# A two-layer encoder on one core: mixer A's empty step taken out, a query split put one step later, and the last half's plain units spread and brought forward

## The chip, the core and the metric

The kernel runs on one core of a Trainium2 chip. The core has a matrix engine (PE in the profile; its weight loads are PEld), a vector engine (DVE), a scalar engine (ACT), a general engine (POOL) and a sync engine (SP) that issues most of the DMAs. Each engine takes its own instructions in order and waits on semaphores for the others. The time is that of one execution in device microseconds. Of the kernel before there are three timed runs and one profiled execution.

## The reference

One sequence of 256 positions, model width 2048, in float32, goes through two layers. Each layer is `h = h + mixer(rms_norm(h))`, then `h = h + conv_ffn(rms_norm(h))`; at the end stands one more RMS norm.

```python
def mixer_a(h, w_qkv, w_o, q_gain, k_gain):      # layer 0
    qkv = h @ w_qkv                               # 16 query heads, 4 key and 4 value heads of 128
    q, k = axial_rope(rms_norm(q, q_gain)), axial_rope(rms_norm(k, k_gain))
    p = softmax(q @ k.T * 128 ** -0.5)            # every query sees every key; 4 query heads share a key head
    return (p @ v) @ w_o

def mixer_b(h, w_qkv, w_o, rel_bias):             # layer 1: 3 groups of 8 heads
    ...                                           # strided windows (128,1), (512,4), (2048,16), a bias by distance
    y = wts[g] * outs[g]                          # groups weighted by their softmax denominators
    return y @ w_o

def conv_ffn(h, w_up, conv_w, conv_b, w_down):
    u = conv3(h @ w_up) + conv_b                  # width 3, one filter for each of 2 x 5632 channels
    gate, val = split(u, 2)
    return (silu(gate) * val) @ w_down
```

The activations are small and the weights are not: nearly all of the work is products of 256 rows with weights that are read once from memory.

## The kernel before

**Products.** Weights come in blocks of 128 x 1024 numbers (512 KB) into one of six `raw` buffers. Each block is split in two: ACT makes the rounded high part `wh` (L128), DVE the rest `wl` (L129, L165 where it goes by halves), both in buffers from a ring of three (four in the down-projection). A product is then three matmuls: high by high, high by low and low by high. A block serves twelve matmuls of 512 columns where it is used plainly. The two splits are moved ahead in the order of the work by 45 instructions (`AHEAD`), so that DVE and ACT take them before other work that is ready.

**Order of the work.** The program is written as one sequence. Helpers that have to run beside the products are Python generators in a list `pending`: after each block, `step()` resumes the first of them up to its next `yield`, and when one ends, the next one is resumed in the same step. A scheduler then makes one in-order queue for each engine; it takes the written order as priority, and takes what it holds to be ready by its own account of durations. So a `yield` more or less moves everything of that generator, and of those behind it, by one block of the product that runs beside it, but the order on an engine need not be exactly the written one.

**Mixer A.** For each of four groups of four query heads, `project` makes the queries from eight blocks (eight steps). Behind it `attend(g)` is started: `qk_post` normalises and rotates the queries (ACT L793 and L903 read the product's banks, DVE L905, L912, L913, POOL L910, and POOL's power at L454 gives the factors `rqk`, which DVE scales at L937). Three steps later PE transposes the queries (L810), ACT and DVE split them into `qTh` and `qTl` (L303, L304). Then come six steps, k = 0 to 5: at k = 0 to 3 the scores of head k are made and their softmax begun ("S", L320 to L322 with `kT` and `qT`, DVE L957, L959, L966, L968, ACT L963), at k = 1 to 4 the probabilities of head k-1 are transposed ("T", L976) and split into `pTh` and `pTl`, and at k = 2 to 5 the output of head k-2 is made ("V", L320 to L322 with `v` and `pT`) and split into the attention's slots `ah` and `al`. Two heads share one bank for V, so the second one's product waits until the first one's output has been read. Between the query split and k = 0 the first group, and it alone, has an empty step; because each generator starts where the one before ends, all four groups keep that place against the products.

**Mixer B.** Six passes (two halves of the heads, three groups) make keys and queries with a Strassen-Winograd scheme (`seven`, seven products in place of eight). Behind each, `k_gen` and `s_gen` turn the keys and queries with the vector engine: a transposition in 32 x 32 blocks (L348), then sixteen block copies, eight on POOL (L358) and eight on ACT (L360), in two steps; one step later, for the first group alone, ACT and DVE split the result into `qTh` and `qTl` (`heads_T_dve`, L303 and L304). After two more steps the scores begin.

**The feed-forward.** The 5632 channels go through in two halves, six and five groups of 512. In the down-projection of a half, the columns are taken in pairs of 512 (0 and 1, then 2 and 3). `weave` writes the order of a pair's units. A plain unit ("c") takes one block and makes twelve matmuls on C11 and C21 (columns n0) or on C12 and C22 (columns n1). A Winograd unit ("P") makes six, from a block that has often been added to another one by DVE first (L248); seven P's do the work of eight c's on one group of channels. The first pair of a half (`late`) begins with LEAD = 4 plain units, because the last group of channels is still being made; at its first use the program empties `pending` (`drain`). After the last P, `combine` (nine operations, ACT L475 and DVE L476 to L487) brings the four product banks M1, M5, M6, M7 into `h`; `done` adds C11 and C21, later C12 and C22 to `h` (DVE L649), and in the last half ACT sums squares (L651) and POOL multiplies by the final gain (L652). All eight banks are in use, and the second pair uses the same ones. The last pair of all (`tail`) has one Winograd group and ends with a plain feed of four products for each bank (L153 to L155), after which the final norm and the stores follow.

Of the kernel before, what the change touches and what calls it, by code (L numbers as in the profile page):

```python
# [28 lines left out]
LEAD = 4  # L29
# [4 lines left out]
def tile_encoder(ctx: ExitStack, tc: tile.TileContext, x, xT, w_a, w_ao, q_gain, k_gain, w_b, w_bo,  # L34
# [34 lines left out]
    def ps_tile():  # L69
        bank_at[1] = (bank_at[1] + 1) % 4  # L70
        return bank(4 + bank_at[1], "ps")
# [12 lines left out]
    def start(gen):  # L84
        if next(gen, StopIteration) is not StopIteration:
            pending.append(gen)
# [414 lines left out]
    def ffn(l, hT, ss_in, g_next, last, side=None):  # L501
        with tc.tile_pool(name=nm("wpool"), bufs=1) as wp, tc.tile_pool(name=nm("fpool"), bufs=1) as fp:
# [101 lines left out]
            for hf, (p0, p1) in enumerate(HALVES):  # L604
# [83 lines left out]
                if last and hf == 1:  # L688
                    for n in range(4):
                        f = hpool.tile([P, 512], F32, tag=f"x{n}", name=nm("fin"))  # L690
                        nc.gpsimd.dma_start(f, final_norm[n * 512:(n + 1) * 512].partition_broadcast(P))
                        fin.append(f)
                def weave(lead, tail):
                    ks = SKG[hf][:1] if tail else SKG[hf]
                    c = [("c", k, i) for k in range(np_) if k not in ks for i in range(4)]
                    ps = [("P", k, p) for k in ks for p in ORDER]
                    if tail:
                        c0, c1 = ([u for u in c if u[2] // 2 == n] for n in range(2))
                        c = c0[:-1] + c1[:3] + c0[-1:] + c1[3:-2]
                    units = []  # L700
                    units += [c.pop(0) for _ in range(lead)]
                    lone = (ps[0], ps[7]) if lead > 1 and hf == 0 else ()
                    for u in ps:
                        units += [u] + [c.pop(0) for _ in range(min(1, len(c))) if u not in lone]
                    return units + c

                hl_ring.insert(0, (wp, 9))
# [8 lines left out]
                    done((a["C11"], a["C21"]), n0)  # L716

                def pair(n0, n1, late, tail=False):
                    units = weave(LEAD if late else 1, tail)
                    late_at = next(i for i, u in enumerate(units) if u[1] == np_ - 1)  # L720
                    acc = project_pair(wd, n0, n1, slots, forms.get, units, late_at if late else None,
                                       lambda a: start(combine(a, n0, n1, fp, "s", combined)),
                                       lambda a: first_half(a, n0, n1), tail=tail)
                    accs = acc["C12"], acc["C22"]
                    if tail:
                        feed(accs, slots, np_ - 1, wd[n1, np_ - 1], False, True, True)
                    done(accs, n1)
                    finished(n0, n1)
# [83 lines left out]
            hi, lo = (v[:, 2 * hp:2 * hp + 2, :].rearrange("p a c -> p (a c)") for v in o)  # L812
            split(hi, lo, t)

    def heads_T_dve(o, s, pool, tag, place="pava"):
        hi, lo = o
        dst = hi if lo is None else s.rearrange("p m c -> p (m c)").rearrange("p (j t) -> p j t", j=4)
        yield from turned(dst, s, pool, tag, place)
        yield
        if lo is not None:  # L820
            split(hi, lo, dst)

    def mixer_a():
        with tc.tile_pool(name="apool", bufs=1) as ap:
# [110 lines left out]
            def attend(g, accs):  # L935
                ro, rq = qk_post(accs, "q")
                nc.vector.tensor_scalar(rq, rq, SCALE, None, op0=ALU.mult)  # L937
                rqv = rq.rearrange("p (m a) -> p m a", m=2)
                qT = pair_tile(ap, [P, 4, NT], "qT")
                yield  # L940
                yield
                yield
                for _ in heads_T(qT, ro):
                    pass
                if g == 0:
                    yield
                prs, pTs, ots = {}, {}, {}
                for k in range(6):
                    yield
                    if k < 4:  # L950
                        i = k
                        s = ps_tile()
                        for m in range(2):
                            mm3(s[:, m * NT:(m + 1) * NT], qT, kT,
                                (slice(None), i, slice(m * P, (m + 1) * P)), (slice(None), g), True, True)
                        mx = small.tile([P, 2], F32, tag="mx", name=nm("mx"), bufs=3)
                        nc.vector.tensor_reduce(mx, s.rearrange("p (m c) -> p m c", m=2), axis=AX.X,  # L957
                                                op=ALU.max, negate=True)
                        nc.vector.tensor_tensor(mx, mx, rqv[:, :, i], ALU.mult)  # L959
                        pr = ap.tile([P, 2, NT], F32, tag="pr", name=nm("pr"), bufs=2)  # L960
                        l = small.tile([P, 2], F32, tag="l", name=nm("l"), bufs=3)
                        for m in range(2):
                            nc.scalar.activation(pr[:, m, :], s[:, m * NT:(m + 1) * NT], AF.Exp,  # L963
                                                 bias=mx[:, m:m + 1], scale=rq[:, 4 * m + i:4 * m + i + 1],
                                                 accum_out=l[:, m:m + 1])
                        nc.vector.reciprocal(l, l)  # L966
                        for m in range(2):
                            nc.vector.tensor_scalar(pr[:, m, :], pr[:, m, :], l[:, m:m + 1], None, op0=ALU.mult)  # L968
                        prs[i] = pr
                    if 1 <= k < 5:  # L970
                        i = k - 1
                        pr = prs.pop(i)
                        t = ps_tile()
                        for m in range(2):
                            for kt in range(2):
                                nc.tensor.transpose(t[:, kt * NT + m * P:kt * NT + (m + 1) * P],  # L976
                                                    pr[:, m, kt * P:(kt + 1) * P], ident)
                        pTs[i] = pair_tile(ap, [P, 2 * NT], "pT", 2)
                        split(pTs[i][0], pTs[i][1], t)
                    if k >= 2:  # L980
                        i = k - 2
                        pT = pTs.pop(i)
                        if i % 2 == 0:
                            ot = ps_tile()
                        j = i % 2
                        for kt in range(2):
                            mm3(ot[:, j * NT:(j + 1) * NT], v, pT,
                                (slice(None), kt, slice(g * P, (g + 1) * P)),
                                (slice(None), slice(kt * NT, (kt + 1) * NT)), kt == 0, kt == 1)
                        hi, lo = slots[4 * g + i]  # L990
                        split(hi, lo, ot[:, j * NT:(j + 1) * NT])
# [41 lines left out]
    def mixer_b(hT, ss_in):  # L1033
        with tc.tile_pool(name="bpool", bufs=1) as bp:
# [26 lines left out]
            for hf in range(2):  # L1061
# [15 lines left out]
                def s_gen(g, accs, bts, nmx=nmx, lsum=lsum, nmv=nmv, probs=probs, e=e, kTs=kTs):  # L1077
                    qs = evac_scaled(bp, accs, rstd)
                    yield
                    yield  # L1080
                    kT, qT = kTs[g], pair_tile(bp, [P, 4, NT], "qT", 1, g > 0)
                    yield from heads_T_dve(qT, qs, bp, "vl", "papa")
                    W = NT if g == 0 else P
                    if g < 2:
                        yield
                    for i in range(4):
                        yield
                        s = ps_tile()
# [16 lines left out]
                        for m in range(2):  # L1105
                            c = 4 * m + i
# [234 lines left out]
```

## Time and profile before

| | |
|---|---|
| time, median of three runs | 2246.29 us (2246.27 to 2246.6) |
| the profiled execution's own time | 2246.85 us |
| its span, first to last instruction | 2245.1 us |
| PE / PEld busy | 2224.6 us (99%) / 1841.5 us (82%) |
| DVE / ACT / POOL busy | 1807.0 us (80%) / 1540.2 us (69%) / 346.3 us (15%) |
| granted TensorE clock | 0.999 |
| read from memory | 429.20 MB, 194 GB/s over the span |

A matmul of 512 columns is recorded as busy for 389 ns on the mean (L154 in the page's groups), but one starts every 227 ns: they overlap. So a wait of PE shows in two ways: as idle time in the record, and, more fully, as the distance between the starts of two neighbours less 227 ns. A row of the timeline has the start, the duration, the engine, the line, the operation, `out<-in` by the program's names, the shape and the count; in square brackets stands the idle time of the engine before it and what ended it.

### The profile page before, as it was taken

The page shows a single profiled execution, that of the slowest core. Times are in us where ns is not written, and L with a number is a line of the kernel's source. Part 1 is how long each engine was busy: PE and PEld are TensorE (multiplying, and loading weights), DVE is VectorE, ACT ScalarE, POOL GpSimd, SP SyncE. Part 2 cuts the span into 40 slices and gives each one's busy share as a digit, 9 for nine tenths or more (in the row PEclk, how much of TensorE's full clock was granted, in tenths as well). Part 3 has the DMA queues.
Part 4 walks back from the last instruction along what each step waited for, and adds up shares of the span by engine and source line. Part 5 has one row for each costly group of instructions (what it writes and reads, how often), then busy time and mean ns, then how long its engine had stood idle before and what let it go on. Part 6 is the DMA issues. An engine that isn't in the chain of part 4 may idle for free.

```text
span 2245.1 us, 29090 instructions
## 1 busy us (share of the span) xinstructions
PE 2224.6 (99%) x10033; PEld 1841.5 (82%) x10033; DVE 1807.0 (80%) x2461; ACT 1540.2 (69%) x2373; POOL 346.3 (15%) x490
## 2 busy tenths in 40 slices
PE   9999999999999999999999999999999999999998
PEld 7888888888888888888888888888888888888876
DVE  6777778888877788979887878786887898688897
ACT  7665777777547777767876777576777755677764
POOL 2211112210001010112340313010110100001101
PEclk9999999999999999999999999999999999999999
DMA  8544656765665665666655565565556566565754
GB/s 302 166 141 141 199 191 212 234 208 188 216 199 187 196 196 174 218 205 210 211 176 192 165 206 178 188 197 188 192 195 193 191 206 208 188 194 189 226 177 150
DMA packets 126499, 437.43 MB, mean 195 GB/s; under 512 B 17312, under 2 KB 18080, under 8 KB 126352
## 3 DMA queue, kind: packets, MB, share of 16 engines
q1 hardware_dynamic: 119744, 425.64, 57.9%
q0 software_dynamic: 6176, 9.39, 1.8%
q8 instruction: 78, 1.28, 0.2%
q14 instruction: 69, 0.57, 0.1%
q10 hardware_dynamic: 432, 0.56, 0.1%
HBM read 429.20 MB, written 6.29 MB: 194 GB/s over the span
## 4 chain that ended last, share of the span: by engine, by line
PE 92%; DVE 3%; POOL 2%; issue 1%; ACT 1%; DMA 1%; SPq 0%; POOLq 0%; DVEq 0%; ACTq 0%
PE acc L155 19%; PE acc L154 19%; PE acc L153 19%; PE acc L288 10%; PE acc L283 10%; PE acc L285 10%; DVE wl L129 1%; POOL stg L358 1%; PE ps L318 1%; POOL pp L358 0%; PE ps L288 0%; PE ps L285 0%; PE ps L320 0%; PE ps L283 0%; PE ps L322 0%
## 5 line engine op out<-in xcount | busy, mean ns | idle before, releaser
L129 DVE TENSOR_TENSOR wl<-raw,wh 128x1024 fp32r<-128x1024 f32 x855 | 1051.3, 1237 | 306.5 <-ACT wh L128 303.3
L128 ACT ACTIVATE wh<-raw 128x1024 fp32r<-128x1024 f32 x855 | 899.3, 1057 | 484.7 <-PE acc L155 200.7
L154 PE MATMUL acc<-wl,xh 128*128 128x512 f32 x1792 | 698.0, 389 | 1.0 <-DVE wl L165 0.7
L153 PE MATMUL acc<-wh,xh 128*128 128x512 f32 x1792 | 698.5, 390 | 0.0
L155 PE MATMUL acc<-wh,xh 128*128 128x512 f32 x1792 | 698.0, 390 | 0.0
L154 PEld LDWEIGHTS acc<-wl,xh 128*128 128x128 f32 x1792 | 336.5, 188 | 71.3 <-DVE wl L165 1.6
L155 PEld LDWEIGHTS acc<-wh,xh 128*128 128x128 f32 x1792 | 336.4, 188 | 69.5
L153 PEld LDWEIGHTS acc<-wh,xh 128*128 128x128 f32 x1792 | 336.4, 188 | 68.9 <-ACT wh L164 0.4
L283 PE MATMUL acc<-wh,ah 128*128 128x512 f32 x762 | 297.1, 390 | 1.9 <-ACT wh L128 1.3
L285 PE MATMUL acc<-wh,al 128*128 128x512 f32 x762 | 296.7, 389 | 0.0
L358 POOL COPY u<-t 32x256 f32<-32x256 f32 x176 | 110.6, 628 | 1003.6 <-DVE t L540 995.5
L288 PE MATMUL acc<-wl,ah 128*128 128x512 f32 x762 | 212.2, 389 | 0.6 <-DVE wl L129 0.6
L283 PEld LDWEIGHTS acc<-wh,ah 128*128 128x128 f32 x762 | 143.0, 188 | 32.6 <-ACT wh L128 1.7
L288 PEld LDWEIGHTS acc<-wl,ah 128*128 128x128 f32 x762 | 142.9, 188 | 30.7 <-DVE wl L129 1.2
L285 PEld LDWEIGHTS acc<-wh,al 128*128 128x128 f32 x762 | 143.0, 188 | 29.5
L360 ACT ACTIVATE u<-t 32x256 f32<-32x256 f32 x352 | 147.8, 420 | 14.1 <-DVE t L540 6.2
L283 PE MATMUL acc<-wh,xh 128*128 128x512 f32 x312 | 122.3, 392 | 1.0 <-ACT wh L128 1.0
L285 PE MATMUL acc<-wh,xh 128*128 128x512 f32 x312 | 121.5, 389 | 0.0
L248 DVE TENSOR_TENSOR raw<-raw,raw 128x1024 f32<-128x1024 f32 x84 | 103.5, 1232 | 14.0 <-DMA raw<-in_w_down_dram 13.1
L288 PE MATMUL acc<-wl,xh 128*128 128x512 f32 x312 | 84.9, 390 | 0.0
L153 PE MATMUL acc<-wh,ah 128*128 128x512 f32 x216 | 84.2, 390 | 0.5 <-DVE cu L478 0.5
L154 PE MATMUL acc<-wl,ah 128*128 128x512 f32 x216 | 84.3, 390 | 0.0
(244 smaller groups left out, 2272.6 us busy)
## 6 DMA issues: line engine op xcount, KB each, us to landing
raw<-in_w_up_dram SPq DMA_DIRECT2D x352, 512.0 KB, 4.4
raw<-in_w_down_dram SPq DMA_DIRECT2D x176, 512.0 KB, 4.8
raw<-in_w_b_dram SPq DMA_DIRECT2D x144, 512.0 KB, 4.5
raw<-in_w_bo_dram SPq DMA_DIRECT2D x48, 512.0 KB, 4.4
raw<-in_w_a_dram SPq DMA_DIRECT2D x40, 512.0 KB, 4.5
raw<-in_w_ao_dram SPq DMA_DIRECT2D x32, 512.0 KB, 3.8
raw<-in_w_a_dram SPq DMA_DIRECT2D x16, 256.0 KB, 6.3
h<-in_x_dram SPq DMA_DIRECT2D x4, 512.0 KB, 8.5
```

Source lines behind the costliest of these rows:

```text
L128: nc.scalar.activation(wh, r, AF.Copy)
L129: nc.vector.tensor_tensor(wl, r, wh.bitcast(F32), ALU.subtract)
L153: nc.tensor.matmul(accs[m], xh, wh[:, j, :], start=st, stop=False)
L154: nc.tensor.matmul(accs[m], xh, wl[:, j, :], start=False, stop=False)
L155: nc.tensor.matmul(accs[m], xl, wh[:, j, :], start=False, stop=sp)
L248: nc.vector.tensor_tensor(dst, dst, src, ALU.add)
L283: nc.tensor.matmul(acc[k], xh, wh[:, j, :], start=k in fresh, stop=False)
L285: nc.tensor.matmul(acc[k], xl, wh[:, j, :], start=False, stop=False)
L288: nc.tensor.matmul(acc[k], xh, wl[:, j, :], start=False, stop=last[k] == i and j == 1)
L318: nc.tensor.matmul(o, lh[ls], rh[rs], start=start, stop=stop)
L358: nc.gpsimd.tensor_copy(dst, src)
L360: nc.scalar.activation(dst, src, AF.Copy)
```

## The change

Four edits.

1. In `attend`, the empty step of the first group is gone.
2. `heads_T_dve` gets a parameter `more`: with it, one more empty step stands between the block copies and the split. `s_gen` sets it for group 0, so in mixer B the two query splits, and the scores behind them, come one step later.
3. `weave` is told `late` of its own. In the first pair of the last half of the last layer, the eight plain units that are left after the first four are spread evenly over the fourteen P's (behind the 2nd, 4th, 6th, 7th, 9th, 11th, 13th and 14th) where they stood behind the first eight. The last plain unit thus stands behind the last P, and the first use of the last channel group moves from behind the fifth P to behind the ninth.
4. The last pair of all begins with four plain units where it began with one. Three fewer stand behind its last P: one before the unit that completes C11 and C21 where there were three, two after it where there were three.

The other pairs keep their order.

```diff
-                def weave(lead, tail):
+                def weave(lead, late, tail):
                     ks = SKG[hf][:1] if tail else SKG[hf]
                     c = [("c", k, i) for k in range(np_) if k not in ks for i in range(4)]
                     ps = [("P", k, p) for k in ks for p in ORDER]
                     if tail:
                         c0, c1 = ([u for u in c if u[2] // 2 == n] for n in range(2))
-                        c = c0[:-1] + c1[:3] + c0[-1:] + c1[3:-2]
+                        c = c0[:-1] + c1[:4] + c0[-1:] + c1[4:-2]
                     units = []
                     units += [c.pop(0) for _ in range(lead)]
-                    lone = (ps[0], ps[7]) if lead > 1 and hf == 0 else ()
-                    for u in ps:
-                        units += [u] + [c.pop(0) for _ in range(min(1, len(c))) if u not in lone]
+                    lone = (ps[0], ps[7]) if late and hf == 0 else ()
+                    rest = len(c)
+                    for i, u in enumerate(ps):
+                        n = min(1, len(c))
+                        if late and hf == 1 and last:
+                            n = (i + 1) * rest // len(ps) - i * rest // len(ps)
+                        units += [u] + [c.pop(0) for _ in range(n) if u not in lone]
                     return units + c
...
                 def pair(n0, n1, late, tail=False):
-                    units = weave(LEAD if late else 1, tail)
+                    units = weave(LEAD if late or tail else 1, late, tail)
...
-    def heads_T_dve(o, s, pool, tag, place="pava"):
+    def heads_T_dve(o, s, pool, tag, place="pava", more=False):
         hi, lo = o
         dst = hi if lo is None else s.rearrange("p m c -> p (m c)").rearrange("p (j t) -> p j t", j=4)
         yield from turned(dst, s, pool, tag, place)
         yield
+        if more:
+            yield
         if lo is not None:
             split(hi, lo, dst)
...
                 for _ in heads_T(qT, ro):
                     pass
-                if g == 0:
-                    yield
                 prs, pTs, ots = {}, {}, {}
...
-                    yield from heads_T_dve(qT, qs, bp, "vl", "papa")
+                    yield from heads_T_dve(qT, qs, bp, "vl", "papa", g == 0)
```

## The prediction

> **What bounds the kernel now.** I read the page's engine lines first, then PE's waits, then the timeline at each wait, and for the last half the busy time by stretches.
>
> ```profile
> span 2245.1 us, 29090 instructions
> PE 2224.6 (99%) x10033; PEld 1841.5 (82%) x10033; DVE 1807.0 (80%) x2461; ACT 1540.2 (69%) x2373; POOL 346.3 (15%) x490
> ```
>
> PE bounds it: 20.5 us of the span are without a matmul. The change adds no matmul and takes none away, so all it can give is a wait of PE, and all it can cost is a new one. PE's waits, longest in total first (columns: us in total, times, longest):
>
> ```profile
> PE ps L320 <- DVE al L304: 3.5, 3, 1.2
> PE acc L283 <- ACT wh L128: 2.3, 2, 1.3
> PE ps L976 <- DVE pr L968: 1.5, 3, 0.5
> ...
> PE acc L283 <- DVE h L649: 0.6, 1, 0.6
> PE acc L288 <- DVE wl L129: 0.6, 1, 0.6
> ...
> PE ps L322 <- DVE qTl L304: 0.2, 1, 0.2
> ```
>
> The first and third stand in mixer A; the last, and one of the two for `wh`, in mixer B; L649, L288 and the other for `wh` in the last half. Each lies beside an edit.
>
> **Edit 1, mixer A.** PE behind the end of group 1's query product (about 100 us), then DVE there:
>
> ```profile
> 106.39 0.40 PE L154 MATMUL acc<-wl,xh 128*128 128x512 f32 x1
> 107.28 0.63 PE L976 MATMUL ps<-ident,pr 128*128 128x128 f32 x4 [0.49 <-DVE pr L968]
> ...
> 110.95 0.39 PE L154 MATMUL acc<-wl,xh 128*128 128x512 f32 x1
> 112.52 0.36 PE L320 MATMUL ps<-pTh,vh 128*128 128x256 f32 x1 [1.18 <-DVE al L304]
> ```
> ```profile
> 105.68 1.19 DVE L913 TENSOR_REDUCE ssq<-sq 128x8 f32<-128x1024 f32 x1
> 106.80 0.60 DVE L968 TENSOR_SCALAR pr<-pr,l 128x256 f32<-128x256 f32 x2
> ...
> 110.13 0.17 DVE L937 TENSOR_SCALAR rqk<-rqk 128x8 f32<-128x8 f32 x1 [1.53 <-POOL rqk L454]
> ...
> 111.96 0.41 DVE L304 TENSOR_TENSOR al<-ps,ah 128x256 fp32r<-128x256 f32 x1
> ```
>
> T and V of head 3 (k = 4 and 5) come one and two blocks behind the end of a product, so behind the next group's `qk_post`. DVE does `qk_post`'s L913 before head 3's probabilities, later stands 1.53 us for POOL's power, and the `al` that V waits for ends at 112.37. From start to start, a pitch being 0.23, T loses 107.28 - 106.39 - 0.23 = 0.66 us and V 112.52 - 110.95 - 0.23 = 1.34 (the recorded idle time is 0.16 short of the loss both times): 2.0 us. The counts of 3 above say that it happens at three such ends: 6.0 us.
>
> Without the empty step all four groups come one block earlier: k = 4 falls on the last step of a product, ahead of the next `qk_post`, and k = 5 one block behind it. There k = 3 and k = 4 stand now, and V of head 2 starts one pitch behind its neighbour, without a wait:
>
> ```profile
> 104.52 0.39 PE L155 MATMUL acc<-wh,xh 128*128 128x512 f32 x1
> 104.75 0.28 PE L320 MATMUL ps<-pTh,vh 128*128 128x256 f32 x1
> ```
>
> So both waits go. Late next is `qTl`: in groups 1 to 3 the query transposition, too, comes nearer to `qk_post`. With V at about 104.75 and two blocks of twelve pitches (2.72 us) behind it, it starts near 110.9 and ends near 111.9, when L937 has been done for 1.6 us; the scores are due one block later, at 114.6, and DVE needs from L937 to the end of `qTl` as long as in group 0 below, 86.68 - 83.2 = 3.5, so until 113.8. That leaves 0.8 us. Bounds of what remains at an end: 0, and 1.4, which is group 0's below; I take 0.3, near the first because of those 0.8. Three ends: 0.9.
>
> Group 0 pays. Its scores move one block forward, from 87.86 to 82.32 + 2.72 = 85.04, their third matmul (the first that reads `qTl`) to about 85.28:
>
> ```profile
> 81.53 1.03 PE L810 MATMUL ps<-ident,ro 128*128 128x128 f32 x8
> 82.32 0.48 PE L153 MATMUL acc<-wh,xh 128*128 128x512 f32 x1
> ...
> 87.86 0.28 PE L320 MATMUL ps<-kTh,qTh 128*128 128x256 f32 x1
> ```
> ```profile
> 83.04 0.17 DVE L937 TENSOR_SCALAR rqk<-rqk 128x8 f32<-128x8 f32 x1 [1.53 <-POOL rqk L454]
> 83.12 2.36 DVE L129 TENSOR_TENSOR wl<-raw,wh 128x1024 fp32r<-128x1024 f32 x2
> 85.40 1.28 DVE L304 TENSOR_TENSOR qTl<-ps,qTh 128x512 fp32r<-128x512 f32 x2
> ```
>
> `qTl` is ready half at 86.1, whole at 86.68: a new wait of 0.8 to 1.4, and I take 1.1. Edit 1: -6.0 + 0.9 + 1.1 = -4.0 us (ends: -6.0 + 0.8 = -5.2, and -6.0 + 4.2 + 1.4 = -0.4).
>
> **Edit 2, mixer B.** ACT and PE at the query splits:
>
> ```profile
> 1039.95 1.06 ACT L303 ACTIVATE qTh<-stg 128x1024 fp32r<-128x1024 f32 x1 [0.70 <-POOL stg L358]
> 1242.49 1.06 ACT L303 ACTIVATE qTh<-stg 128x1024 fp32r<-128x1024 f32 x1 [1.55 <-POOL stg L358]
> 1243.45 1.04 ACT L128 ACTIVATE wh<-raw 128x1024 fp32r<-128x1024 f32 x1
> ```
> ```profile
> 1242.98 0.61 PE L288 MATMUL acc<-wl,xh 128*128 128x512 f32 x2
> 1244.55 0.50 PE L283 MATMUL acc<-wh,xh 128*128 128x512 f32 x1 [0.95 <-ACT wh L128]
> ```
>
> The split stands at the head of ACT's queue until POOL's copies end; the `wh` that PE waits for is queued behind it. From start to start PE loses 1244.55 - 1242.98 - 0.46 (two pitches) = 1.11 us. At the first split it loses the 0.2 for `qTl` in the list of waits and again 0.16. One step later, 1.36 us of PE behind a P or 2.72 behind a plain unit, the copies are over or nearly. The scores keep their two steps from the split and come later by one; nobody stands waiting for their softmax, which is used after all three groups. No DMA moves. Bounds: -1.47, and +0.8 if a bank taken in another turn costs what the one wait for a bank now costs (L649, 0.64 + 0.16). I take -1.2, near the first, whose place the rows show.
>
> **Edits 3 and 4, the last half.** Busy time by stretches (columns: PE, PEld, DVE, ACT, POOL, clock, DMA share, GB/s): four plain units; eight pairs of P and plain unit; P's alone; the seam to the last pair; two stretches of the last pair.
>
> ```profile
> 2128.00:2138.90 10.90, 10.90 (x50) 9.02 (x49) 9.95 (x15) 10.65 (x19) 2.58 (x4) 1.00 0.50 171
> 2138.90:2171.50 32.60, 32.60 (x145) 27.02 (x144) 29.18 (x33) 18.49 (x22) 0.00 (x0) 1.00 0.56 184
> 2171.50:2180.00 8.50, 8.50 (x39) 7.03 (x38) 8.50 (x9) 6.02 (x8) 1.05 (x1) 1.00 0.60 194
> 2180.00:2194.00 14.00, 11.45 (x49) 8.50 (x47) 14.00 (x17) 7.61 (x12) 6.20 (x4) 1.00 0.30 108
> 2194.00:2211.80 17.80, 17.80 (x78) 14.56 (x79) 16.02 (x15) 9.03 (x10) 0.98 (x1) 1.00 0.71 232
> 2211.80:2236.50 24.70, 24.66 (x109) 20.08 (x107) 17.08 (x23) 8.01 (x11) 4.93 (x3) 1.00 0.25 88
> ```
>
> From where the P's stand alone DVE is full, 22.5 of 22.5 us, and at the seam PE has the three waits of the list, 1.3 + 0.6 + 0.6 and three times 0.16: 3.0 us. DVE's operations there, by groups:
>
> ```profile
> L248 DVE TENSOR_TENSOR raw<-raw,raw 128x1024 f32<-128x1024 f32 x9 | 11.0, 1217 | 1.5 <-DMA raw<-in_w_down_dram 1.5
> L649 DVE TENSOR_TENSOR h<-acc,h 128x512 f32<-128x512 f32 x4 | 2.6, 678 | 0.0
> ```
>
> A P gives PE six pitches, 1.36 us, and asks DVE for a split (1.2, the two at 83.12 in 2.36) and four times in seven for an L248 (1.2); a plain unit gives 2.72 and asks 1.2. Six P's at the end: 8.2 us of PE, 6 x 1.2 + 4 x 1.2 = 12.0 of DVE. Spread, two P's and a plain unit give 5.4 and ask 3.6 + 1.4 = 5.0; the four plain units ahead of the last pair give 10.9 and ask 4.8, which frees 6 us of DVE just where `combine` and `done` (twelve operations like L649's, 8.1) fall due. DVE was idle 0.95 + 3.42 us in the first two stretches, which the spread order can use. Against it: 5.0 in 5.4 leaves little for the last group's filter work, and C21, which the last pair's first unit needs, is complete only one plain unit ahead. The wait that is left lies between 0 and 4 (8.1 of DVE in the 2.72 + 1.36 between the last two P's and the seam); I take 1.0, as the four early units bring most of the slack: -2.0 (ends -3.0 and +1.0). The later drain costs 0, hidden by four more P's. SP's loads follow the units: plain units ask 0.52 MB in 2.72 us, 193 GB/s, and the last pair has run at 232 with no wait of PE.
>
> At the very end four units and the feed, 16.3 us, follow the last P where 24.5 did. Due in them: seven operations of `combine` (4.8), C11 and C21 (1.4), some six splits (7.2), 13.4, which fits; POOL's multiplies (within its 4.93) start 2.7 us later, with 10.9 left. Cost 0, bounds 0 and 1.
>
> **Sum.** -4.0 - 1.2 - 2.0 = -7.2. The profiled execution took 2246.85 us, its span and 1.75 around it: 2239.65. It stands 0.56 over the median of the runs; against that, 2239.1. About 0.2%, 4.5 us, is what a measurement of this kernel can tell from no change.
>
> **Rivals.** *The wait moves on (same).* At each end in mixer A `wl` and `qTl` lose what V gains: DVE's queue keeps its length, only its order differs. For it: PE gains 2.0 us at each end, by which every split is due sooner. Against: the 0.8 above. Edit 1 gives 0: 2246.3 - 3.2 = 2243.1.
>
> *The order doesn't follow (same).* The queues are the scheduler's: the row at 107.28 has T in the middle of a block. If it keeps scores, T and V where they stand, edits 1 and 2 give nothing, 3 and 4 half: 2245.3. Against: those rows recur three times, at the same place of each group, as the written steps do.
>
> *Slower.* L937's wait for POOL gets in front of `qTl` in all four groups: 1.5 idle, two splits (2.4) and `qTl` (1.3) are 5.2 us between transposition and scores, where 2.72 of products stand: 2.5 lost in each, 10. Slower beyond 0.2% it is from (9.2 + 4.5) / 4 = 3.4 each, when the products' own `wl` is held, too. At 3.6: 2246.3 - 9.2 + 14.4 = 2251.5. For it: group 0 shows this queue. Against: groups 1 to 3 have a V more in front.
>
> *POOL's copies grow (faster, by less).* In mixer B, with ACT no longer held, more `wl` run beside the copies:
>
> ```profile
> 1234.35 8.11 POOL L358 COPY stg<-tT 32x256 f32<-32x256 f32 x8 [1.64 <-DVE tT L348]
> 1030.17 9.75 POOL L358 COPY stg<-tT 32x256 f32<-32x256 f32 x8 [1.40 <-DVE tT L348]
> ```
>
> The same eight copies take 8.11 or 9.75 us. At 9.75 the second split's end 1.64 later, more than a P's step; ACT stands as long as now, and edit 2 gives 0: 2240.3. [...]
>
> **How the numbers follow.** Forecast 0.50, growing copies 0.08, wait moves on 0.22, order doesn't follow 0.11, slower 0.09: faster 0.58, same 0.33, slower 0.09. The lower end is all three waits gone for nothing, 2246.3 - 6.0 - 1.5 - 3.0 = 2235.8; the upper one reaches over the two same cases, 2245.8.
>
> **What would show it.** Edit 1: L320 <- al and L976 <- pr gone from PE's waits, one for `qTl` near 85 us. Edit 2: no ACT idle for POOL before `qTh`. Edits 3 and 4: DVE below 100% ahead of the seam, its three waits under 1.5 us in sum. I am wrong if waits for `qTl` or `wl` in mixer A sum to over 3 us, or if DVE is full from 2140 us on and PE waits at the drain.

## The result, and the profile after

The changed kernel took 2241.01 us in the median of eleven runs (2239.1 to 2243.7); the kernel before, beside it, 2246.29 (2245.55 to 2247.34). The ratio is 0.9975, with a 95% interval of 0.9967 to 0.9983: faster by 5.3 us, a quarter of a per cent. The prediction was 2239.1, with a range of 2235.8 to 2245.8. The profiled execution took 2241.01 us, 5.84 less than the one before. Of the runs further down one, with edit 4 alone, took 4197.44 us at a mean granted clock of 0.527, and the ratio given for edit 4 leaves it out.

The page's line of the engines (span 2239.2 us), and PE's waits (us in total, times, longest):

```profile
PE 2224.3 (99%) x10033; PEld 1842.0 (82%) x10033; DVE 1804.9 (81%) x2461; ACT 1540.5 (69%) x2373; POOL 341.6 (15%) x490
```
```profile
PE acc L283 <- DVE h L649: 1.5, 1, 1.5
...
PE acc L283 <- ACT wh L128: 1.1, 2, 1.0
PE ps L322 <- DVE qTl L304: 0.6, 1, 0.6
```

The work is the same; what has changed is the list of waits. `al` (3.5 us, three times) and `pr` (1.5, three times) are gone, and `qTl` is new at 0.6: that is edit 1. The 0.2 for `qTl` in mixer B is gone with edit 2, and 0.16 for `wh` stands in its place. The 0.95 for `wh`, which edit 2 was to remove, is still in the 1.1. At the seam of the last half one wait of 1.5 for `h` stands where three stood.

For the stretches I use the starts of PE's n-th matmul of 512 columns, whose order is nearly the same in all kernels here. A stretch before is taken from the same stretch after:

| stretch, by count of 512-column matmuls | before, us | after, us | difference |
|---|---|---|---|
| 200 to 1000: mixer A's groups and a little more | 223.69 | 218.71 | -4.98 |
| 4000 to 5600: mixer B's six passes | 384.73 | 384.71 | -0.02 |
| 8000 to 9480: most of the last half | 339.04 | 337.67 | -1.37 |
| all the rest, start and end of the program included | 1299.39 | 1299.92 | +0.53 |

Their sum is the 5.84 us of the two profiled executions. The last line is outside of what the edits move. In the fourteen traces of this document it lies between 1298.2 and 1299.9 us, so 0.5 us is what two executions differ by there.

In mixer A, PE after the change at the place of the former waits, and at group 0's scores, with DVE there:

```profile
102.79 0.39 PE L155 MATMUL acc<-wh,xh 128*128 128x512 f32 x1
103.19 0.63 PE L980 MATMUL ps<-ident,pr 128*128 128x128 f32 x4
...
106.89 0.39 PE L155 MATMUL acc<-wh,xh 128*128 128x512 f32 x1
107.11 0.28 PE L320 MATMUL ps<-pTh,vh 128*128 128x256 f32 x1
```
```profile
85.39 0.28 PE L321 MATMUL ps<-kTl,qTh 128*128 128x256 f32 x1
86.27 0.39 PE L322 MATMUL ps<-kTh,qTl 128*128 128x256 f32 x1 [0.60 <-DVE qTl L304]
```
```profile
83.18 0.17 DVE L943 TENSOR_SCALAR rqk<-rqk 128x8 f32<-128x8 f32 x1 [1.53 <-POOL rqk L454]
83.26 2.36 DVE L129 TENSOR_TENSOR wl<-raw,wh 128x1024 fp32r<-128x1024 f32 x2
85.53 1.28 DVE L304 TENSOR_TENSOR qTl<-ps,qTh 128x512 fp32r<-128x512 f32 x2
```

The transposition T loses 103.19 - 102.79 - 0.23 = 0.17 us where it lost 0.66; V, one block later, follows at 0.22, the pitch, and loses nothing where it lost 1.34. Group 0 pays 86.27 - 85.39 - 0.12 (the pitch of 256 columns) = 0.76. DVE still stands 1.53 us for POOL's power, and two splits `wl`, then `qTl`, queue behind it.

In mixer B, ACT's wait for POOL and PE's wait for `wh` at the second split are as before, to the hundredth:

```profile
1237.89 1.06 ACT L303 ACTIVATE qTh<-stg 128x1024 fp32r<-128x1024 f32 x1 [1.55 <-POOL stg L358]
```
```profile
1239.95 0.50 PE L283 MATMUL acc<-wh,xh 128*128 128x512 f32 x1 [0.95 <-ACT wh L128]
```
```profile
1025.62 9.75 POOL L358 COPY stg<-tT 32x256 f32<-32x256 f32 x8 [1.40 <-DVE tT L348]
1229.75 8.11 POOL L358 COPY stg<-tT 32x256 f32<-32x256 f32 x8 [1.64 <-DVE tT L348]
```

In the last half, busy time by stretches (columns: PE, PEld, DVE, ACT, POOL, clock, DMA share, GB/s): the spread units; the last of them up to the seam. Then DVE ahead of the one wait:

```profile
2133.30:2165.90 32.60, 32.60 (x145) 26.99 (x145) 32.44 (x38) 20.22 (x25) 0.00 (x0) 1.00 0.52 169
2165.90:2178.00 12.10, 10.68 (x48) 8.51 (x46) 11.49 (x15) 6.34 (x8) 1.40 (x1) 1.00 0.90 310
```
```profile
2174.97 0.68 DVE L481 TENSOR_TENSOR cu<-acc,cu 128x512 f32<-128x512 f32 x1
2175.57 0.68 DVE L482 TENSOR_TENSOR h<-h,cu 128x512 f32<-128x512 f32 x1
2176.17 0.68 DVE L484 TENSOR_TENSOR h<-h,cu 128x512 f32<-128x512 f32 x1
2176.77 0.68 DVE L486 TENSOR_TENSOR cu<-acc,cu 128x512 f32<-128x512 f32 x1
2177.37 0.68 DVE L649 TENSOR_TENSOR h<-acc,h 128x512 f32<-128x512 f32 x1
```
```profile
2176.20 0.39 PE L285 MATMUL acc<-wh,al 128*128 128x512 f32 x1
2178.10 0.50 PE L283 MATMUL acc<-wh,ah 128*128 128x512 f32 x1 [1.52 <-DVE h L649]
```

The spread order fills DVE: 32.44 of 32.60 us (29.18 before). The seam is left with one wait, 2178.10 - 2176.20 - 0.23 = 1.67 us, in place of three that lost 3.0. The first unit of the last pair writes the bank of C11 or C21, which L649 has to read first; ahead of that read, DVE's queue has the combination (L478 to L486), whose result that unit doesn't need.

### The profile page after: what moved, and what is told of

It reads as the page before. It is cut to its first block, busy times and chain, and to the rows that moved or that the text cites. A ratio compares the mean times of both kernels' runs of the same rounds, so it can differ in the third digit from the quotient of the medians.

```text
span 2239.2 us, 29097 instructions
## 1 busy us (share of the span) xinstructions
PE 2224.3 (99%) x10033; PEld 1842.0 (82%) x10033; DVE 1804.9 (81%) x2461; ACT 1540.5 (69%) x2373; POOL 341.6 (15%) x490
```

## The experiments

The times are medians of 5 to 11 runs unless said otherwise, each beside the kernel before on the same chip, whose medians were 2246.83, 2247.49 and 2246.93 us in the three groups below.

### Each edit alone

Edit 1 alone:

```diff
-                if g == 0:
-                    yield
```

> The kernel before with only mixer A's empty step taken out. Theory read from the two traces, the parts add: the n-th 512-column matmul comes 4.1 to 4.7 us earlier from the middle of mixer A on, so this kernel takes about 4.7 us less than before (2241.6 against 2246.3). By the prediction's own sum it would be 4.0 less (2242.3), with about 1 us lost at one new wait for qTl in group 0. Rival, the parts lean on each other (the gain of A is partly lost later unless the last half's order is changed too): less than 3.5 us. In the profile: the waits at L320 for al and at L976 for pr gone, one wait at L322 for qTl of 0.5 to 0.9 us near 86 us, mixer B and the last half as before.

2241.96 us, ratio 0.9979 (0.9971 to 0.9988): 4.9 less. Matmul 200 to 1000 took 218.68 us, as in the changed kernel (218.71). The wait for `qTl` is 0.76 again, and no other came. So the edit gives about 4.9, the additive reading holds, and the prediction's 4.0 was too careful.

Edit 2 alone:

```diff
...
         yield from turned(dst, s, pool, tag, place)
         yield
+        if more:
+            yield
         if lo is not None:
             split(hi, lo, dst)
...
```

> The kernel before with only mixer B's first split written one step later. Theory read from the two traces: each engine's queue is put in order by the times the scheduler reckons, and the later place in the text does not move the split in ScalarE's queue; so qTh still waits about 1.5 us for the copy stg of GpSimd, TensorE still waits about 1.0 us behind it near 1245 us, and the time is as before within 0.4 us (2245.9 to 2246.7). Rival, the prediction's term: 1.2 us less (2245.1), both waits gone. In the profile the two differ in ScalarE's idle time ahead of qTh in group 0 of either half: 1.55 and 0.72 by the first, under 0.3 by the second.

2247.02 us, ratio 1.0001 (0.9992 to 1.0009). ACT and PE in its trace:

```profile
1241.27 1.06 ACT L303 ACTIVATE qTh<-stg 128x1024 fp32r<-128x1024 f32 x1 [1.55 <-POOL stg L358]
```
```profile
1243.33 0.50 PE L283 MATMUL acc<-wh,xh 128*128 128x512 f32 x1 [0.95 <-ACT wh L128]
```

Both waits are whole, and matmul 4000 to 5600 took 384.71 us against 384.73. At the first split PE loses 0.30 us for `wh` where it lost 0.36 for `qTl`. Edit 2 gives nothing that the times could show.

Edit 3 alone (the spread), and edit 4 alone:

```diff
...
-                    for u in ps:
-                        units += [u] + [c.pop(0) for _ in range(min(1, len(c))) if u not in lone]
+                    rest = len(c)
+                    for i, u in enumerate(ps):
+                        n = min(1, len(c))
+                        if late and hf == 1 and last:
+                            n = (i + 1) * rest // len(ps) - i * rest // len(ps)
+                        units += [u] + [c.pop(0) for _ in range(n) if u not in lone]
...
```

> The kernel before with only the usual units of the last half's first pair spread evenly. Edits 3 and 4 together moved the time by 1.4 to 1.8 us between the two traces. Theory A: it is the spread that empties the stretch ahead of the seam of its waits, so alone it gives 1.4 us or more (2244.9 or less), and the three waits of TensorE at the seam, 3.04 us in sum before, come to 1.7 or less. Theory B: the spread only fills VectorE (99.5 per cent busy from 2133 to 2166 us after the change, against some 90 before) and the gain is that of the four units that stand first in the last pair; alone it gives between 0.5 less and 1.5 more than before (2245.8 to 2247.8). If the wider scatter of the changed kernel's runs (4.6 us from least to most, 1.8 before) comes from the spread, this kernel's runs scatter by more than 3 us.

```diff
-                        c = c0[:-1] + c1[:3] + c0[-1:] + c1[3:-2]
+                        c = c0[:-1] + c1[:4] + c0[-1:] + c1[4:-2]
...
-                    units = weave(LEAD if late else 1, tail)
+                    units = weave(LEAD if late or tail else 1, tail)
```

> The kernel before with only the last pair's four usual units first (and its order of usual units to match). Theory A (the spread does it): alone within 0.5 us of before (2245.8 to 2246.8). Theory B (the four units first do it): 1.4 us less or better (2244.9 or less), with the sum of TensorE's waits at the seam, 3.04 us before, at 1.7 or less, since four units of work that need no P unit's result cover the last combine of the first pair. Scatter of runs as before (under 2 us) unless this edit is the cause of the wider scatter.

Edit 3: 2245.57 us, ratio 0.9995 (0.9986 to 1.0004); edit 4: 2246.42, ratio 0.9998 (0.9988 to 1.0007). Neither can be told from no change, and neither reaches the 1.4 that its theory asked for. Each leaves one longer wait at the seam in place of three. PE with edit 3, then with edit 4:

```profile
2181.31 0.39 PE L288 MATMUL acc<-wl,ah 128*128 128x512 f32 x1
2183.54 0.50 PE L283 MATMUL acc<-wh,ah 128*128 128x512 f32 x1 [1.85 <-DVE h L649]
```
```profile
2184.27 0.62 PE L288 MATMUL acc<-wl,ah 128*128 128x512 f32 x2
2187.13 0.50 PE L283 MATMUL acc<-wh,ah 128*128 128x512 f32 x1 [2.24 <-DVE h L649]
```

That is 2.0 and 2.4 us from start to start (in edit 4's trace about 1.6 more went with the clock, an estimate of the last section). From matmul 8000 to 9480 edit 3 alone took 337.87 us, 1.2 less than before; edit 4 alone took 339.63, and 338.0 without those 1.6, 1.0 less. Both together took off 1.4. So both theories fall as they were put, which ask which of the two edits does it: by this stretch of one trace each, either does most of it alone, the two gains don't add, and the wait for L649 is left by both. Edit 3's runs lie 4.0 us apart; but the 33 runs of the kernel before lie 3.4 apart beside them, so the scatter tells nothing here.

### The waits that the change leaves

All of these stand on the changed kernel, which was run again beside them.

> The changed kernel once more, so that the next three kernels have it on the same chip. Theory: about 5.3 us under before (2241.0 when before is 2246.3). In some executions of the two kernels with one of edits 3 and 4 alone and of edit 1 alone the granted clock fell to half for 3 to 4 us right after the seam's wait (1.5 to 1.7 us lost); if that chance is what scatters the changed kernel's runs, they lie in two groups about 1.6 us apart, or spread over 3 us and more again.

2240.85 us, 6.6 less than before, ratio 0.9969 (0.9958 to 0.9981), from 2239.43 to 2242.57. The seam's wait was 2.10 us in its trace (1.94 recorded idle), 1.67 in the first one; in the five traces with the changed order at this seam (these two, and below SCALE, the four copies and the five steps) the recorded idle time lies between 1.41 and 2.30. The scatter of 3 us is there again, but not in two groups.

SCALE folded into the power's argument, since SCALE x^-1/2 = (128 x)^-1/2:

```diff
-    def rsqrt_mean(dst, ss, n):
+    def rsqrt_mean(dst, ss, n, by=1.0):
...
-        nc.vector.tensor_scalar(ms, ss, 1.0 / n, EPS, op0=ALU.mult, op1=ALU.add)
+        nc.vector.tensor_scalar(ms, ss, by / n, by * EPS, op0=ALU.mult, op1=ALU.add)
...
-                rsqrt_mean(r, ssq, P)
+                rsqrt_mean(r, ssq, P, P if which == "q" else 1.0)
...
-                nc.vector.tensor_scalar(rq, rq, SCALE, None, op0=ALU.mult)
```

> The changed kernel with the query's SCALE folded into the argument of GpSimd's power, so that VectorE has no scaling of rqk any more and does not stand 1.53 us for the power at the head of its queue. Theory (group 0's new wait comes from that stand): the wait for qTl near 86 us, 0.76 us from start to start, goes; VectorE has the 1.5 us in all four groups, but only group 0's path uses it: 0.5 to 0.9 us under the changed kernel. Rival (the wait comes from the two splits of wl that stand ahead of qTl, the stand only ends in them): under 0.2 us, the wait stays above 0.5.

2239.27 us, 1.6 under the changed kernel beside it. DVE and PE at group 0:

```profile
82.74 1.23 DVE L129 TENSOR_TENSOR wl<-raw,wh 128x1024 fp32r<-128x1024 f32 x1 [0.17 <-ACT wh L128]
83.88 1.28 DVE L304 TENSOR_TENSOR qTl<-ps,qTh 128x512 fp32r<-128x512 f32 x2
```
```profile
85.17 0.28 PE L321 MATMUL ps<-kTl,qTh 128*128 128x256 f32 x1
85.29 0.28 PE L322 MATMUL ps<-kTh,qTl 128*128 128x256 f32 x1
```

DVE no longer stands for POOL, `qTl` ends at 85.16, 1.6 us earlier than in the changed kernel (0.2 of it because PE was that much ahead in this execution), and PE loses nothing. From matmul 300 to 700 that is 126.76 us against 127.54: 0.78, the wait's own size. So the stand behind the power made the wait. The other 0.8 of the medians' difference has no place in the trace; it lies within the scatter.

Four of POOL's eight copies given to ACT, for mixer B's first split:

```diff
-                    yield from heads_T_dve(qT, qs, bp, "vl", "papa", g == 0)
+                    yield from heads_T_dve(qT, qs, bp, "vl", "paaa" if g == 0 else "papa", g == 0)
```

> The changed kernel with mixer B's first query split (group 0 of either half) fed by four block copies on GpSimd instead of eight, ScalarE taking the other four (0.42 us each). Theory (the copies on GpSimd, 1.3 us each beside VectorE's work, are what holds the split, and its written place is not): ScalarE's wait of 1.55 us before qTh goes, GpSimd's four copies are done some 4 us earlier, and TensorE's 1.11 and 0.32 us behind it go: 1.0 to 1.4 us under the changed kernel, which is what edit 2 was to bring. Rival (ScalarE's four further copies, 1.7 us, take the place of the wait): within 0.4 us of the changed kernel, with wh late by as much as before.

2241.32 us, 0.5 over the changed kernel beside it: no gain. POOL's copies, and ACT:

```profile
1230.24 4.40 POOL L358 COPY stg<-tT 32x256 f32<-32x256 f32 x4 [1.64 <-DVE tT L348]
```
```profile
1238.14 1.06 ACT L128 ACTIVATE wh<-raw 128x1024 fp32r<-128x1024 f32 x1
1239.11 0.58 ACT L1194 ACTIVATE ms<-ps 128x512 f32<-128x512 f32 x1
1239.70 0.41 ACT L360 ACTIVATE stg<-tT 32x256 f32<-32x256 f32 x1
1240.20 1.06 ACT L303 ACTIVATE qTh<-stg 128x1024 fp32r<-128x1024 f32 x1
```

POOL is done at 1234.64, as the theory had it, but ACT's own last copy has moved behind two other instructions, and `qTh` starts at 1240.20 instead of 1237.89. The rival holds in the time: ACT's copies are as late as POOL's were. PE's 1.11 for `wh` is down to 0.17, but a little later it loses 0.61 for `wl`, and matmul 4000 to 5600 took 385.23 us against 384.71.

C11 and C21 of the first pair added to `h` ahead of the rest of the combination:

```diff
+                            if n > 0:
-                            nc.vector.tensor_tensor(hs, accs[m], hs, ALU.add)
+                                nc.vector.tensor_tensor(hs, accs[m], hs, ALU.add)
...
+                    if hf == 1 and last and n0 == 0:
+                        add_residual((a["C11"], a["C21"]), n0)
                     if hf == 1:
                         finished(n0, n1)
```

> The changed kernel with C11 and C21 of the last half's first pair added to h at once, ahead of the rest of the combination, instead of behind it (the sums are the same, in another order). Theory (the one wait left at the seam is VectorE's queue: the bank that the last pair's first unit needs stands behind operations that need not come first): TensorE's wait for h, 1.68 us from start to start at 2178 us, falls under 0.4, no half clock follows it, 1.2 to 1.7 us under the changed kernel, and the runs scatter less (under 3 us). Rival (VectorE is simply full there, so the wait moves to a later unit of the last pair): within 0.5 us of the changed kernel, with new waits of TensorE between 2180 and 2195 us that sum to over 1 us.

2238.87 us, 2.0 under the changed kernel beside it, and its five runs lie within 0.4 us. DVE and PE at the seam (L493 is the addition that L649 made):

```profile
2174.86 0.68 DVE L493 TENSOR_TENSOR h<-acc,h 128x512 f32<-128x512 f32 x1
2175.46 0.67 DVE L481 TENSOR_TENSOR cu<-acc,cu 128x512 f32<-128x512 f32 x1
```
```profile
2174.96 0.39 PE L285 MATMUL acc<-wh,al 128*128 128x512 f32 x1
2175.59 0.50 PE L283 MATMUL acc<-wh,ah 128*128 128x512 f32 x1 [0.24 <-DVE h L493]
```

The wait is 2175.59 - 2174.96 - 0.23 = 0.40, no new one follows, and matmul 8000 to 9480 took 336.00 us against 337.67. DVE is as full as before; only the order of its queue has changed. Of the two additions only the second moved, ahead of four operations of the combination; the first stood early already (2167.5 in the changed kernel, 2167.4 here). That is the theory.

### The split's place, the gains together, and what edits 3 and 4 are worth

The split written five steps later instead of one (one execution):

```diff
-        if more:
-            yield
+        for _ in range(5 if more else 0):
+            yield
```

> The changed kernel with mixer B's first split written not one but five steps later. Theory (the scheduler puts the split where it reckons its inputs ready, and the written place has no say): ScalarE's queue is in the same order around qTh of group 0 in both halves, its wait for GpSimd's copy is again 1.5 us near 1238 us, TensorE loses again about 1.1 us near 1240 us. Rival (one step was too short a way, five are enough): the split behind the next one or two wh, no wait of ScalarE for GpSimd, TensorE's 1.1 us gone. One look, so the time says little: 2239 to 2243 by either.

```profile
1238.04 1.06 ACT L303 ACTIVATE qTh<-stg 128x1024 fp32r<-128x1024 f32 x1 [1.55 <-POOL stg L358]
```
```profile
1240.10 0.50 PE L283 MATMUL acc<-wh,xh 128*128 128x512 f32 x1 [0.95 <-ACT wh L128]
```

2241.45 us. `qTh` has the same neighbours in ACT's queue with no step, one step and five. The scores behind it did move as written: in the first half of the heads the first of them stands behind the 4369th matmul of 512 columns before, the 4381st with one step, the 4435th with five, and `qTh` starts behind the 4362nd in all of them. The written place has no say over the split here.

SCALE in the power and the early addition together, and then with the copies shared four (POOL), eight (ACT), four (DVE):

> The changed kernel with both SCALE in the power and C11 and C21 added early. Theory (the two waits stand in different stages and add): the 0.76 us of group 0 and 1.3 to 1.7 us of the seam both gone, 2.1 to 2.5 us under the changed kernel, that is 7.4 to 8.6 us under before; the runs lie within 1 us of each other. Rival (one of the two gains is lost downstream): no better than the early residual alone, 8.6 us under before when measured beside it but 6.8 to 7.3 by the trace.

```diff
-                    yield from heads_T_dve(qT, qs, bp, "vl", "papa", g == 0)
+                    yield from heads_T_dve(qT, qs, bp, "vl", "pava" if g == 0 else "papa", g == 0)
```

> As the kernel with both, and the block copies of mixer B's first query split shared four on GpSimd, eight on ScalarE, four on VectorE (before: eight and eight). ScalarE's queue then keeps its order and its load. Theory (GpSimd's eight copies, 8.1 and 9.8 us, hold the split): GpSimd done some 4 us earlier, ScalarE's waits of 1.55 and 0.72 us before qTh gone, TensorE's 1.11 and 0.30 behind them gone: 1.0 to 1.4 us under the kernel with both. Rival (VectorE, which does the splits wl at the same time, is made late by four copies more): within 0.5 us, a wait of TensorE for wl in the place of that for wh.

With both: 2238.06 us, ratio 0.9958 (0.9944 to 0.9971), 8.9 under before; group 0's wait is gone, the seam has 0.75 us. Its runs lie 2.2 us apart, so neither the sum nor the narrow scatter of the early addition alone is sharp, and 8.9 is hardly more than the 8.6 of the early addition beside its own before. That both gains are there is seen in the trace: 0.8 us less than the changed kernel in matmul 200 to 1000, 1.3 less in 8000 to 9480. With the copies shared: 2236.70, ratio 0.9952 (0.9939 to 0.9964), 10.2 under before. POOL, ACT and DVE in mixer B, with the copies shared:

```profile
1227.71 4.40 POOL L358 COPY stg<-tT 32x256 f32<-32x256 f32 x4 [1.64 <-DVE tT L348]
```
```profile
1234.52 1.06 ACT L303 ACTIVATE qTh<-stg 128x1024 fp32r<-128x1024 f32 x1 [0.21 <-DVE stg L362]
```
```profile
1233.22 1.19 DVE L362 COPY stg<-tT 32x256 f32<-32x256 f32 x4
```

Four copies cost DVE 1.19 us together. ACT's queue has the order that it had, its wait is 0.21 instead of 1.55, and PE waits for `wh` nowhere. Matmul 4000 to 5600 took 383.15 us against 384.63 with both: 1.48, and the prediction's bound for edit 2 was 1.47. So the mechanism that the prediction saw (POOL's copies hold the split, the split holds `wh`) is right, and shorter copies remove it where a later step does not. This kernel has the lowest time here.

The kernel with both, less edits 2, 3 and 4:

> The kernel before with edit 1 alone, SCALE in the power and C11 and C21 added early: the kernel with both, less edits 2, 3 and 4. Theory (edits 3 and 4 gave what they gave by shortening the wait for the bank of C11, which the early residual takes away by itself): within 0.5 us of the kernel with both, TensorE's waits at the seam under 0.8 us in sum. Rival (the four units first and the spread give slack of their own): 1 us or more over the kernel with both, with waits for h, wl or cu of over 1 us left between 2165 and 2195 us.

2240.06 us, 2.0 over the kernel with both. PE, then DVE, after the seam:

```profile
2184.39 0.39 PE L283 MATMUL acc<-wh,ah 128*128 128x512 f32 x1
2186.43 1.19 PE L288 MATMUL acc<-wl,ah 128*128 128x512 f32 x4 [1.64 <-DVE wl L129]
...
2190.39 0.96 PE L288 MATMUL acc<-wl,ah 128*128 128x512 f32 x3 [0.27 <-DVE wl L129]
```
```profile
2182.42 1.73 DVE L487 TENSOR_TENSOR h<-h,cu 128x512 f32<-128x512 f32 x1
2184.07 2.30 DVE L129 TENSOR_TENSOR wl<-raw,wh 128x1024 fp32r<-128x1024 f32 x1
```

The early addition takes the wait for the bank away by itself (0.20 us is left of it), but without edits 3 and 4 the wait moves on: PE then stands 1.8 and 0.4 us for `wl`. DVE does the combination there beside P units that need their splits twice as often, and it is slow besides: L487 takes 1.73 us where it took 0.68 in the changed kernel, the split 2.30 where others took 1.22, both while POOL multiplies by the final gain (2182.30 to 2183.60 and 2183.87 to 2185.29). These 2.1 us are nearly as much as PE loses, and no run here takes the multiplies away, so how much the order of the units does by itself stays open. In the changed kernel splits beside the multiplies are slow as well (two took 3.94 us from 2182.55 on, two 2.35 from 2191.55 on, after the multiplies), and PE, in its plain units, doesn't wait. So edits 3 and 4 give room of their own, the rival's case. In the changed kernel part of that room is lost to the order of DVE's queue.

## Why the prediction was right, and where it was not

**The sum.** Predicted -7.2, measured -5.3 in the medians and -5.8 in the profiled executions. Two terms were off in opposite directions, and one was wrong: by the traces edit 1 gave 0.9 more than its term, edits 3 and 4 some 0.6 less, edit 2 nothing of its 1.2. That the sum came within 1.9 us of the median is partly luck, as the first of these covers half of the others.

**Edit 1: right, a little low.** The mechanism is what the rows show: V loses 0 and T 0.17 us at each of the three ends, where I had taken 0.3; group 0's new wait is 0.76, where I had taken 1.1, between 0.8 and 1.4. That makes -6.0 + 0.5 + 0.8 = -4.7, and 4.9 to 5.0 was measured. The 0.76 is the lower bound's case: the first half of `qTl` is all that head 0's scores need, and no second wait follows. The rivals "the wait moves on" and the slower one are out: nothing in mixer A waits longer than 0.76, although DVE's stand behind POOL is the cause of that one, as the slower rival had it for all four groups.

**Edit 2: wrong.** Its sign, no idle time of ACT before `qTh`, was missed with 1.55 us. The step that failed is "One step later, 1.36 us of PE behind a P or 2.72 behind a plain unit, the copies are over or nearly". It takes for granted that the split moves in ACT's queue when it moves in the program. It does not: not by one step, not by five. This is the rival "the order doesn't follow", which I gave 0.11 and put against edits 1 and 2 together, because mixer A's rows recur as the written steps do. It has to be asked place by place: in mixer A the order followed, in mixer B it did not. That the scheduler reckons the copies shorter than they are (in the changed kernel 1.3 us each beside DVE's splits, 0.4 at 1235.53 and 1235.96, where DVE is idle), and so holds the split to be ready earlier than it is, would explain it; no run shows the scheduler's account, and this stays argued. The rival "POOL's copies grow" gave the same zero for another reason; the copies took 9.75 and 8.11 us in both kernels, so it is out.

**Edits 3 and 4: right in kind, smaller in size.** -2.0 was predicted, with 1.0 us of waits left of 3.0. One wait of 1.67 is left in the first trace of the changed kernel and 2.10 in the second, and matmul 8000 to 9480 gained 1.37. The five traces with this seam took 337.4 to 338.1 us there, against 339.0 and 339.5 in the two without edits 3 and 4 that kept the full clock, so the gain lies between 1.0 and 2.1. The medians alone, 5.3 and 6.6 less with all edits and 4.9 with edit 1, each beside its own before, say only that it is small. The sign "under 1.5 us in sum" was missed, and that "the four early units bring most of the slack" isn't borne out: alone they took off 1.0, the spread alone 1.2. My calculation weighed DVE's work against PE's time and found it to fit; it didn't look at the order in which DVE does it. Four operations of the combination stand in front of the one read that frees the bank. DVE below 100% ahead of the seam was named as a sign; it was at 99.5% in the spread stretch, and PE didn't wait there once. A full DVE was the wrong sign to watch; the place of the one needed operation in its queue was the right one.

**The end.** The tail was put at 0: from matmul 9480 to the last instruction it was 10.59 us before and 10.59 after.

## What to carry to other kernels

When an edit moves a step in the program, look first whether the engine's own queue follows; where it doesn't, shorten the operation that is late (here four copies moved to DVE, 1.48 us) instead of writing its reader later. When an engine is full ahead of a seam, sort its queue by who waits: one addition brought forward past four others took 1.3 to 1.7 us from a wait that more room had only shortened, but the room was needed, too: without it the kernel was 2.0 us slower. And a small scaling (0.17 us) that stood for POOL's power at the head of DVE's queue cost DVE 1.53 us and PE 0.78 in the changed kernel's group 0: fold such a scaling into what the other engine computes.

## What was not expected of the hardware

After the seam's waits the granted clock fell to half in two of the fourteen traces: with edit 1 alone and with edit 4 alone. The busy time by stretches there (columns as above), first edit 1, then edit 4:

```profile
2182.50:2186.50 4.00, 4.00 (x11) 3.14 (x12) 4.00 (x5) 2.86 (x6) 1.76 (x2) 0.57 0.00 0
```
```profile
2188.20:2191.50 3.30, 3.30 (x9) 2.61 (x8) 2.59 (x4) 2.15 (x4) 2.35 (x2) 0.50 0.02 9
```

From 2186.50 and from 2191.50 us on the clock was 1.00 again. With edit 1 the mean of 0.57 over 4.00 us comes to 3.4 us at half; with edit 4 the whole 3.30 us of the row are at half. With edit 4 two matmuls in a row took 0.62 us at 2184.27 and 1.05 at 2188.22: they start about every 427 ns instead of 227, as the first ones of the trace before do from 2.05 to 5.46 us. An estimate from these numbers of what it costs each time: 3.4 x (1 - 227/427) = 1.6 us.

With edit 1 PE had waited 1.10 and 0.62 us within 3 us ahead of the fall, with edit 4 2.24. In two further traces, with the four copies and with the five steps, the seam's recorded idle time was 2.30 and 2.29 us, and the clock was 1.00 all through (2160 to 2200 us). So in these traces the length of the idle time alone doesn't tell whether the clock falls: 1.72 us in two waits were followed by a fall, 2.30 in one were not. What decides it, no run here shows.

So in two of the fourteen traces the seam's wait was followed by a further loss, by that estimate 1.6 us each. Whether that makes the changed kernel's scatter of 3 to 4.6 us stays open: the early addition alone, with 0.40 us of wait, had runs within 0.4 us, but the two kernels built on it, with waits of 0.75 and 0, had 2.2 and 1.9.
